# A hybrid decoder layer: steps of the recurrence, the convolution and its norm given out a slot or an operation apart, and small diagonals made on ScalarE

## The chip, the cores and the metric

The kernel runs on one core of a Trainium2 chip. The metric is device microseconds of one execution. A core has TensorE (PE; its weight loads are shown as PEld), VectorE (DVE), ScalarE (ACT), GpSimd (POOL) and SyncE (SP, which starts the transfers here). Each engine works through its own instructions in the order in which they stand; an instruction waits for semaphores of others, and all behind it on that engine wait with it. The matrix products accumulate in PSUM banks; everything else lies in SBUF.

## The reference

One layer on 512 tokens of 1024 channels, all in fp32. Three sub-layers follow one another: a SwiGLU block (inner width 2816, added at half weight), a token mixer, and a second SwiGLU block. Each takes `u = x*(1+scale)+shift` and gives `x <- LayerNorm(alpha*x + w*(1+gate)*f(u))`; scale, shift and gate come from a conditioning vector c. The mixer is where most of the change lies:

```python
proj = u @ w_in                                   # 6 parts of 1024
xr, gr, conf_in, gate_a, gate_b = jnp.split(proj, IN_SPLITS, axis=-1)
xr = causal_depthwise_conv(xr, rnn_conv_w, rnn_conv_b)            # 4 taps
hr = rg_lru(xr, ...)                              # two 128x128 products a head, then a scan
ya = (hr * jax.nn.gelu(gr)) @ rnn_w_proj
glu = conf_in[..., :D_CONV] * jax.nn.sigmoid(conf_in[..., D_CONV:])
hb = causal_depthwise_conv(glu, conf_dw_w, conf_dw_b)             # 31 taps
hb = jax.nn.silu(layer_norm(hb, conf_ln_g, conf_ln_b))
yb = hb @ conf_w_proj
out = (jax.nn.sigmoid(gate_a) * ya + jax.nn.sigmoid(gate_b) * yb) @ mix_w_out
```

The recurrence of `rg_lru` is `h_t = a_t*h_(t-1) + sqrt(1-a_t^2)*(i_t*x_t)`, with `a = exp(-8 softplus(-lambda) r)` and sigmoid gates r and i.

## The kernel before, in words

**Tiling.** Channels lie on the 128 partitions, the 512 tokens in the free dimension, so 1024 channels are eight chunks. Every fp32 product is made of three in a faster 32-bit format: high by high (L240), low by high (L241), high by low (L242). A group of one output chunk is eight chunks of weights by three products, 24 matmuls of 128x512. A weight slab comes by transfer into `raw` (two buffers); ScalarE casts the high part `whi` (L141), and the low part `wlo = raw - whi` (L145) is made on VectorE, or on GpSimd in the boundaries and the mixer (`lo_engine`). These are made four and three groups ahead (`HI_AHEAD`, `LO_AHEAD`). Activations are split the same way into `Uh`, `Ul` or `Hh`, `Hl`.

**Stages.** Startup; FFN1; boundary l1; mixer; boundary l2; FFN2; `finish` (l3 and the output). A boundary makes the last four chunks of the sub-layer's output in two halves of 256 tokens each (`Tail`; tiles `l1t`, `l2t`, `l3t`), and meanwhile the LayerNorm of the half that is done. That norm sums over channels by a product with a constant matrix (`l_rs` L317, `l_mean`), takes the inverse deviation `l_y` on GpSimd, spreads it over a diagonal matrix (`l_dg`, `diagonals`, L341), and broadcasts it by a product with ones (`l_rs` L448).

**The mixer.** It goes in four pairs of chunks. In each pair come two groups `xr` (evicted by ScalarE at L1049, and three taps on VectorE at L1053, the third of which frees the PSUM bank), the recurrence of the pair before (`rglru`: four `ri` products, then steps on VectorE, L989, L996, L1000, L1002, L1006, and ScalarE, L983, L992, L993, L997), `cb` and `ca` (the convolution's input), and two groups `gr`. Then follow 16 gate groups (`gate` into `ma` and `sb`), eight groups `ya`, eight groups `yb`. The 31-tap convolution is 30 VectorE operations per chunk (`cv`, L841) on an accumulator in PSUM; ScalarE starts it (L821) and copies it out (L846). Two accumulators are under way at a time. When all eight are out, `conv_norm` makes their LayerNorm: the sum over channels (`lc_sum`, then `lc_mu` on TensorE, L880), centring (L888), squares (L890), their sum (L894), `lc_y`, `lc_dg` (L341), `lc_rs` on TensorE (L908), scaling (L914), SiLU (L918).

**What sets the order.** The program is written out by hand, engine by engine in the order of the Python calls. Before each group, `slot()` gives out the work that was deferred for that slot (`defer(n, f)`: n slots later), then the casts ahead. Each half group is a `checkpoint()`, which first gives out the `quick` list (an entry `(n, f)` waits n further checkpoints) and then, in `background()`, spends a budget of credit on the convolution's taps and, when there are none, on the list `later`. Nothing reorders the instructions afterwards on an engine.

## Time and profile before

| | |
|---|---|
| median of 3 runs | 1182.73 us (1182.71 to 1182.8) |
| the profiled execution | 1182.73 us, of which its span 1180.9 us |
| TensorE busy | 1154.6 us |
| VectorE busy | 749.1 us |
| ScalarE busy | 434.0 us |
| GpSimd busy | 216.6 us |
| boundary l1, mixer, boundary l2 | from about 345 us, 425 us and 770 us of the span |

In a row of a timeline stand the start, the duration, the engine, the line, the operation, the tile written and those read, their shape, and in brackets the idle time before it with what ended it. A start is counted from the beginning of the span. In a row of windows stand the stretch and its length, the busy time of PE, PEld, DVE, ACT and POOL with the number of instructions, the clock that TensorE was granted (1.00 is full), the share of the transfer engines and GB/s.

### The profile page before, as it was taken

The page shows a single profiled execution, that of the slowest core. Times are in us where ns is not written, and L with a number is a line of the kernel's source. Part 1 is how long each engine was busy: PE and PEld are TensorE (multiplying, and loading weights), DVE is VectorE, ACT ScalarE, POOL GpSimd, SP SyncE. Part 2 cuts the span into 40 slices and gives each one's busy share as a digit, 9 for nine tenths or more (in the row PEclk, how much of TensorE's full clock was granted, in tenths as well). Part 3 has the DMA queues.
Part 4 walks back from the last instruction along what each step waited for, and adds up shares of the span by engine and source line. Part 5 has one row for each costly group of instructions (what it writes and reads, how often), then busy time and mean ns, then how long its engine had stood idle before and what let it go on. Part 6 is the DMA issues. An engine that isn't in the chain of part 4 may idle for free.

```text
span 1180.9 us, 13555 instructions
## 1 busy us (share of the span) xinstructions
PE 1154.6 (98%) x5527; PEld 970.4 (82%) x5527; DVE 749.1 (63%) x1030; ACT 434.0 (37%) x557; POOL 216.6 (18%) x112
## 2 busy tenths in 40 slices
PE   8999999999999999998999999999999999999996
PEld 5888888888888988887788878889888888888886
DVE  7887767732359596998999665596433232433266
ACT  4532122322323635566653442225322122222223
POOL 3200000000003554353536440022300000000002
PEclk9999999999999999998999999999999999999998
DMA  9787666422322222332233222221422321322212
GB/s 371 268 344 281 261 266 244 170 103 107 107 72 108 72 81 81 107 113 75 81 107 112 103 72 107 85 94 37 143 75 103 107 93 59 134 107 75 103 36 72
DMA packets 30318, 151.64 MB, mean 128 GB/s; under 512 B 3376, under 2 KB 5424, under 8 KB 18480
## 3 DMA queue, kind: packets, MB, share of 16 engines
q1 hardware_dynamic: 30256, 150.78, 34.9%
q8 instruction: 43, 0.70, 0.2%
q14 instruction: 19, 0.16, 0.0%
HBM read 148.67 MB, written 2.10 MB: 128 GB/s over the span
## 4 chain that ended last, share of the span: by engine, by line
PE 83%; DVE 9%; issue 3%; ACT 2%; POOL 1%; DMA 1%; SPq 0%; POOLq 0%; ACTq 0%; DVEq 0%
PE g L240 6%; PE u L240 6%; PE g L242 6%; PE u L242 6%; PE g L241 6%; PE u L241 6%; PE y L240 6%; PE y L241 6%; PE y L242 6%; PE st L759 4%; PE gate L240 2%; PE gate L242 2%; PE gate L241 2%; DVE cv L841 2%; PE yb L241 1%
## 5 line engine op out<-in xcount | busy, mean ns | idle before, releaser
L145 POOL TENSOR_TENSOR wlo<-raw,whi 128x1024 fp32r<-128x1024 f32 (+1 forms) x69 | 170.2, 2482 | 555.4 <-ACT whi L141 555.4
L141 ACT CAST whi<-raw 128x1024 fp32r<-128x1024 f32 (+2 forms) x204 | 205.4, 1021 | 151.9 <-DMA raw<-in_wide 116.0
L841 DVE SCALAR_TENSOR_TENSOR cv<-glu,prm,cv 128x511 f32<-128x511 f32 (+14 forms) x240 | 159.0, 729 | 12.5 <-ACT cv L821 12.5
L145 DVE TENSOR_TENSOR wlo<-raw,whi 128x1024 fp32r<-128x1024 f32 (+1 forms) x135 | 158.2, 1190 | 4.7 <-ACT whi L141 4.7
L689 DVE TENSOR_TENSOR h<-u,h 128x512 f32<-128x512 f32 x38 | 26.3, 691 | 204.7 <-PE u L242 204.7
L241 PE MATMUL y<-Hl,whi 128*128 128x512 f32 x320 | 124.5, 389 | 0.0
L242 PE MATMUL y<-Hh,wlo 128*128 128x512 f32 x320 | 124.5, 389 | 0.0
L240 PE MATMUL y<-Hh,whi 128*128 128x512 f32 x320 | 124.5, 389 | 0.0
L240 PE MATMUL g<-Uh,whi 128*128 128x512 f32 x304 | 118.3, 389 | 0.0
L241 PE MATMUL g<-Ul,whi 128*128 128x512 f32 x304 | 118.3, 389 | 0.0
L242 PE MATMUL g<-Uh,wlo 128*128 128x512 f32 x304 | 118.3, 389 | 0.0
L240 PE MATMUL u<-Uh,whi 128*128 128x512 f32 x304 | 118.3, 389 | 0.0
L241 PE MATMUL u<-Ul,whi 128*128 128x512 f32 x304 | 118.3, 389 | 0.0
L242 PE MATMUL u<-Uh,wlo 128*128 128x512 f32 x304 | 118.3, 389 | 0.0
L141 ACT CAST Hh<-h 128x512 fp32r<-128x512 f32 x44 | 27.0, 620 | 178.1 <-DVE h L689 178.1
L257 DVE SCALAR_TENSOR_TENSOR ada<-ada,silu_c 128x1024 f32<-128x1024 f32 x72 | 86.6, 1224 | 4.8 <-DMA ada<-in_ada 4.7
L242 PEld LDWEIGHTS y<-Hh,wlo 128*128 128x128 f32 x320 | 60.1, 188 | 12.5
L240 PEld LDWEIGHTS y<-Hh,whi 128*128 128x128 f32 x320 | 60.1, 188 | 12.5
L241 PEld LDWEIGHTS y<-Hl,whi 128*128 128x128 f32 x320 | 60.1, 188 | 12.5
L334 POOL TENSOR_TENSOR l_y<-l_va,half 128x2 f32<-128x2 f32 x5 | 3.5, 706 | 359.3 <-DVE l_va L333 359.3
L685 ACT ACTIVATE h<-g 128x512 f32<-128x512 f32 x38 | 22.7, 597 | 120.4 <-PE g L242 120.4
L242 PEld LDWEIGHTS g<-Uh,wlo 128*128 128x128 f32 x304 | 57.1, 188 | 11.9
(260 smaller groups left out, 2333.3 us busy)
## 6 DMA issues: line engine op xcount, KB each, us to landing
raw<-in_wide SPq DMA_DIRECT2D x92, 1024.0 KB, 4.8
ada<-in_ada SPq DMA_DIRECT2D x72, 512.0 KB, 7.3
raw<-in_six SPq DMA_DIRECT2D x8, 768.0 KB, 4.1
straw<-in_start SPq DMA_DIRECT2D x8, 512.0 KB, 8.9
X<-in_xT SPq DMA_DIRECT2D x8, 256.0 KB, 9.0
out_y<-X SPq DMA_DIRECT2D x8, 256.0 KB, 2.2
raw<-in_rg SPq DMA_DIRECT2D x4, 256.0 KB, 2.6
silu_c<-in_c SPq DMA_DIRECT2D x1, 512.0 KB, 3.5
```

Of the source, the lines that this page charges most:

```text
L141: self.nc.scalar.copy(out=out, in_=src)
L145: (engine or self.nc.vector).tensor_tensor(out=out, in0=src, in1=hi.bitcast(F32), op=ALU.subtract)
L240: t.matmul(ps, lhsT=w[0], rhs=x[0], start=first, stop=False)
L241: t.matmul(ps, lhsT=w[0], rhs=x[1], start=False, stop=False)
L242: t.matmul(ps, lhsT=w[1], rhs=x[0], start=False, stop=last)
L257: self.nc.vector.scalar_tensor_tensor(out=raw, in0=raw, scalar=1.0, in1=self.sc, op0=ALU.mult, op1=ALU.mult, accum_out=self.mod[:, j : j + 1])
L334: self.nc.gpsimd.tensor_tensor(out=y, in0=va, in1=self.half[:, :nb], op=ALU.pow)
L685: self.nc.scalar.activation(out=h, in_=pg, func=AF.Silu)
L689: self.nc.vector.tensor_tensor(out=h, in0=pu, in1=h, op=ALU.mult)
L759: nc.tensor.matmul(ps[i], lhsT=w[k][a][:, i * P : (i + 1) * P], rhs=self.U[b][:, k, :], start=k == 0 and (a, b) == (0, 0), stop=k == KC - ...
L841: self.nc.vector.scalar_tensor_tensor(out=acc[:, n:], in0=glu[:, : T - n], scalar=self.col("conf_dw_w", c, NTAP - 1 - n), in1=acc[:, n:], ...
```

## The change

Five things are done. (1) In `ln_front`, at the group m = 3, the fourth `wlo` of the tail that follows is asked for at once. (2) The tails' diagonals are made by ScalarE, one 128x128 activation for each block, two for a half; in `finish` the diagonal of the second half stands ahead of a subtraction, and one output operation goes from ScalarE to GpSimd. (3) A convolution that has had its last tap is copied out two convolution steps later, and only then is the next one begun. (4) The recurrence's four steps become seven, a slot apart, with the scan a checkpoint behind the square root. (5) In `conv_norm` centring, squares and sums, and later scaling and SiLU, are given out in turn, and `lc_rs` a checkpoint later.

```diff
     def diagonals(self, nm, y, scalar=False):
         nb = y.shape[1]
         dg = self.pair(f"{nm}_dg")[:, 0, :].rearrange("p (a b) -> p a b", a=4)[:, :nb, :]
+        if scalar:
+            for i in range(nb):
+                self.nc.scalar.mul(out=dg[:, i, :], in_=self.ident, mul=y[:, i : i + 1])
+            return dg
         self.nc.vector.tensor_tensor(out=dg, in0=self.ident.unsqueeze(1).broadcast_to([P, nb, P]),
...
             def diagonal(self_, h):
-                st[h]["dg"] = self.diagonals(f"{name}{h}", st[h]["y"])
+                st[h]["dg"] = self.diagonals(f"{name}{h}", st[h]["y"], scalar=True)
...
-        out(0, 3, (act, act))
+        out(0, 3, (act, pool))
+        t.diagonal(1)
         t.sub(1, 0)
-        t.diagonal(1)
         t.broadcast(1)
...
             self.group(ps, w, x)
+            if m == 3:
+
+                self.lo_to(self.cur + 3)
             if m == 2:
...
             self.after.pop(self.steps)()
-        ready = [a for a in self.active if self.active_from[a[0]] <= self.steps] or self.active
+        a = self.ending.pop(self.steps, None)
+        if a in self.active:
+            self.conv_end(a)
+            while self.waiting and len(self.active) < 2:
+                self.conv_begin()
+        live = [a for a in self.active if a[3] < NTAP - 1]
+        if not live:
+            self.conv_end(self.active[0])
+            return True
+        ready = [a for a in live if self.active_from[a[0]] <= self.steps] or live
...
         if n == NTAP - 1:
-            self.nc.scalar.copy(out=self.conv_out(c), in_=acc)
-            self.active.remove(a)
-            self.done.append(c)
-            p = c // 2
-            if {2 * p, 2 * p + 1} <= set(self.done) and p < 3:
-                self.after[self.steps + 3] = lambda: self.conv_sum(p)
+
+            self.ending[self.steps + 2] = a
         return True
+
+    def conv_end(self, a):
+        c, _, acc, _ = a
+        self.nc.scalar.copy(out=self.conv_out(c), in_=acc)
+        self.active.remove(a)
+        self.done.append(c)
+        p = c // 2
+        if {2 * p, 2 * p + 1} <= set(self.done) and p < 3:
+            self.after[self.steps + 3] = lambda: self.conv_sum(p)
...
         def centre(p):
             v.tensor_tensor(out=CV[p], in0=CV[p], in1=self.over(st["mu"], 2), op=ALU.subtract)
+
+        def square(p):
             st[f"q{p}"] = self.pair(f"lc_q{p}")
             nc.scalar.activation(out=st[f"q{p}"], in_=CV[p], func=AF.Square)
+
+        def gather(p):
+            v.tensor_tensor(out=st["q0"], in0=st["q0"], in1=st[f"q{p}"], op=ALU.add)
+        self.later(1.14, lambda: centre(0))
         for p in range(4):
-            self.later(1.14, lambda p=p: centre(p))
-            if p:
-                self.later(1.14, lambda p=p: v.tensor_tensor(out=st["q0"], in0=st["q0"], in1=st[f"q{p}"], op=ALU.add))
+            if p < 3:
+                self.later(1.14, lambda p=p: centre(p + 1))
+            self.later(0.0, lambda p=p: square(p))
+            if p > 1:
+                self.later(1.14, lambda p=p: gather(p - 1))
+        self.later(1.14, lambda: gather(3))
...
-            self.quick.append((0, bc))
+            self.quick.append((1, bc))
...
-        def a():
+        def gated():
             v.tensor_tensor(out=xc, in0=xc, in1=i_, op=ALU.mult)
+
+        def decay():
...
-        def b():
+        def power():
             v.scalar_tensor_tensor(out=th, in0=i_, scalar=1.0, in1=th, op0=ALU.add, op1=ALU.mult)
+
+        def root():
             s.activation(out=th, in_=th, func=AF.Sqrt)
-
-        def c():
+            self.quick.append((1, scan))
+
+        def scan():
             v.tensor_tensor(out=xc, in0=xc, in1=th, op=ALU.mult)
...
-        def e():
+        def out():
             v.tensor_tensor(out=i_, in0=i_, in1=gg, op=ALU.mult)
-            self.hi(hi, i_)
-            self.defer(1, lambda: self.lo(lo, i_, hi))
-
-        for n, fn in enumerate((a, b, c, e)):
-            self.defer(n + 2, fn)
+
+        for n, fn in enumerate((gated, decay, power, root, out, lambda: self.hi(hi, i_), lambda: self.lo(lo, i_, hi))):
+            self.defer(n + 1, fn)
```

How the instructions of an engine stand before and now is shown at three places; line numbers of the changed kernel are its own (L868 is the copy of L846, L828 the start of L821, L1088 the eviction of L1049, L857 the tap of L841, L1025 the multiplication of L989).

ScalarE, the fourth pair of the mixer, before. `xc` is the eviction of the first `xr` group, `Hh<-i` the cast of the recurrence's result of an earlier pair, `CV<-cv` a finished convolution copied out, `cv<-glu` the start of the next.

```order
L1065 ACTIVATE gg_3699<-gr 128x512 x2
L141 CAST Hh<-i_3751 128x1024
L141 CAST whi_3972<-raw_3855 128x1024
L141 CAST whi_3976<-raw_3931 128x1024
L846 COPY CV_3999<-cv_3456 128x512
L1049 ACTIVATE xc_3967<-xr,prm 128x512
L821 ACTIVATE cv_4015<-glu_3280,prm 128x512
L846 COPY CV_3999<-cv_3460 128x512
L821 ACTIVATE cv_4020<-glu_3280,prm 128x512
L983 ACT_TABLE_LOAD
```

The same place now:

```order
L1104 ACTIVATE gg_3701<-gr 128x512 x2
L141 CAST whi_3973<-raw_3857 128x1024
L141 CAST whi_3977<-raw_3930 128x1024
L1088 ACTIVATE xc_3969<-xr,prm 128x512
L868 COPY CV_4016<-cv_3459 128x512
L828 ACTIVATE cv_4018<-glu_3282,prm 128x512
L868 COPY CV_4016<-cv_3477 128x512
L828 ACTIVATE cv_4023<-glu_3282,prm 128x512
L141 CAST Hh<-i_3753 128x1024
L1018 ACT_TABLE_LOAD
```

The eviction `xc` has moved ahead of both copies and of the cast, which stands behind the copies and starts.

VectorE, the same pair a little later, before: `Hl<-i` and `Hl<-xc` are the low parts of the recurrence's result and of the new `xc`, `xc<-xc,i` the gate multiplication of the recurrence.

```order
L145 TENSOR_TENSOR Hl<-i_3751,Hh 128x1024
L866 TENSOR_TENSOR lc_sum<-CV_3442,CV_3999 128x1024
L841 SCALAR_TENSOR_TENSOR cv_4015<-glu_3280,prm,cv_4015 128x510
L1053 SCALAR_TENSOR_TENSOR xc_3967<-xr,prm,xc_3967 128x511
L841 SCALAR_TENSOR_TENSOR cv_4020<-glu_3280,prm,cv_4020 128x510
L1053 SCALAR_TENSOR_TENSOR xc_3967<-xr,prm,xc_3967 128x510
L841 SCALAR_TENSOR_TENSOR cv_4015<-glu_3280,prm,cv_4015 128x509
L1053 SCALAR_TENSOR_TENSOR xc_3967<-xr,prm,xc_3967 128x509
L841 SCALAR_TENSOR_TENSOR cv_4020<-glu_3280,prm,cv_4020 128x509
L145 TENSOR_TENSOR Hl<-xc_3967,Hh 128x1024
L841 SCALAR_TENSOR_TENSOR cv_4015<-glu_3280,prm,cv_4015 128x508
L989 TENSOR_TENSOR xc_3698<-xc_3698,i_4027 128x1024
```

Now:

```order
L887 TENSOR_TENSOR lc_sum<-CV_3457,CV_4016 128x1024
L857 SCALAR_TENSOR_TENSOR cv_4018<-glu_3282,prm,cv_4018 128x509
L1092 SCALAR_TENSOR_TENSOR xc_3969<-xr,prm,xc_3969 128x510
L857 SCALAR_TENSOR_TENSOR cv_4023<-glu_3282,prm,cv_4023 128x509
L1092 SCALAR_TENSOR_TENSOR xc_3969<-xr,prm,xc_3969 128x509
L857 SCALAR_TENSOR_TENSOR cv_4018<-glu_3282,prm,cv_4018 128x508
L145 TENSOR_TENSOR Hl<-i_3753,Hh 128x1024
L1025 TENSOR_TENSOR xc_3700<-xc_3700,i_4029 128x1024
L145 TENSOR_TENSOR Hl<-xc_3969,Hh 128x1024
L857 SCALAR_TENSOR_TENSOR cv_4023<-glu_3282,prm,cv_4023 128x508
```

The low part `Hl<-i` has moved behind the taps of `xc`, and the gate multiplication between the two low parts.

VectorE at the end of FFN1, ahead of the tail, before. `l_s` and `l_q` are the sums of X and of its squares, the five `drv` rows small columns of eight; the product `l1t` waits for the second `wlo`.

```order
L145 TENSOR_TENSOR wlo_2426<-raw_2324,whi_2390 128x1024
L665 SCALAR_TENSOR_TENSOR X<-y,drv,X 128x512
L679 TENSOR_TENSOR l_s_2455<-X 128x1024
L680 TENSOR_TENSOR l_q_2454<-l_q_2454,l_q_2456 128x1024
L295 SCALAR_TENSOR_TENSOR drv<-mod,prm 128x8
L296 SCALAR_TENSOR_TENSOR drv<-mod,prm 128x8
L297 TENSOR_TENSOR drv<-drv,mod 128x8
L298 TENSOR_SCALAR drv<-prm 128x8
L299 TENSOR_SCALAR drv<-prm 128x8
L145 TENSOR_TENSOR wlo_2466<-raw_2324,whi_2424 128x1024
L366 SCALAR_TENSOR_TENSOR X<-l1t_2468,drv,X 128x256
```

Now:

```order
L145 TENSOR_TENSOR wlo_2426<-raw_2324,whi_2390 128x1024
L145 TENSOR_TENSOR wlo_2453<-raw_2324,whi_2424 128x1024
L672 SCALAR_TENSOR_TENSOR X<-y,drv,X 128x512
L686 TENSOR_TENSOR l_s_2457<-X 128x1024
L687 TENSOR_TENSOR l_q_2456<-l_q_2456,l_q_2458 128x1024
L295 SCALAR_TENSOR_TENSOR drv<-mod,prm 128x8
```

The second `wlo` has moved directly behind the first, and the update, the sums and the `drv` rows behind it.

More of the change, by code (lines that the diff above doesn't have):

```diff
@@ L110, in __init__ @@
         self.active_from, self.last_step, self.steps = {}, {}, 0
-        self.done, self.after = [], {}
+        self.done, self.after, self.ending = [], {}, {}
         self.CV = [None] * 4
@@ L335, in deviation, with diagonals @@
         return y
-    def diagonals(self, nm, y):
+    def diagonals(self, nm, y, scalar=False):
         nb = y.shape[1]
         dg = self.pair(f"{nm}_dg")[:, 0, :].rearrange("p (a b) -> p a b", a=4)[:, :nb, :]
+        if scalar:
+            for i in range(nb):
+                self.nc.scalar.mul(out=dg[:, i, :], in_=self.ident, mul=y[:, i : i + 1])
+            return dg
         self.nc.vector.tensor_tensor(out=dg, in0=self.ident.unsqueeze(1).broadcast_to([P, nb, P]),
@@ L914, in scale, with silu @@
             v.tensor_tensor(out=CV[p], in0=CV[p], in1=self.over(st["rs"], 2), op=ALU.mult)
+        def silu(p):
             for j in range(2):
@@ L925, in conv_norm @@
         ends = []
+        self.later(1.14, lambda: scale(0))
         for p in range(4):
-            self.later(1.14, lambda p=p: scale(p))
+            if p < 3:
+                self.later(1.14, lambda p=p: scale(p + 1))
+            self.later(0.0, lambda p=p: silu(p))
         self.until(free)
```

## The prediction

> **What bounds the kernel now.** I read the page first, then the waits of TensorE, then the timelines of the four engines around each wait.
>
> ```profile
> span 1180.9 us, 13555 instructions
> PE 1154.6 (98%) x5527; PEld 970.4 (82%) x5527; DVE 749.1 (63%) x1030; ACT 434.0 (37%) x557; POOL 216.6 (18%) x112
> ```
>
> TensorE is busy for 98% of the span, and the change takes no product from it. What can be won is the time in which it waits, or runs at a lower clock; what can be lost is a new wait. The profiled execution took 1182.73 us, which is also the median of the three runs; 1.83 us of it lie around the span.
>
> ```profile
> PE l_rs L448 <- DVE l_dg L341: 4.6, 3, 2.8
> PE cb L240 <- DVE xc L1053: 3.5, 1, 3.5
> PE lc_rs L908 <- DVE lc_dg L341: 1.4, 1, 1.4
> PE l_rs L317 <- DVE l_sum L381: 1.1, 2, 0.6
> PE l1t L242 <- DVE wlo L145: 1.0, 1, 1.0
> PE l2t L242 <- DVE wlo L145: 1.0, 1, 1.0
> PE gate L240 <- ACT ma L1078: 0.7, 1, 0.7
> ```
>
> The columns are the total, the number of waits and the longest, in us. These seven lines add to 13.3 us, and every part of the change stands beside one of them: the weight half `wlo` at the boundaries, the broadcast diagonals `l_dg`, the recurrent branch's `xc` that holds back `cb`, and the broadcast `lc_rs`. I go through them in that order of the program, and follow each to the wait that comes after it, for a wait that is removed only lets TensorE reach the next one sooner.
>
> **Boundaries (l1, and l2 alike).** The fourth `wlo` of the tail now goes to VectorE ahead of the update of X, the sums and five small `drv` operations.
>
> ```profile
> 358.25 0.28 PE L241 MATMUL l1t<-Hl,whi 128*128 128x256 f32 x1
> 359.53 0.38 PE L242 MATMUL l1t<-Hh,wlo 128*128 128x256 f32 x1 [1.00 <-DVE wlo L145]
> ...
> 365.01 0.28 PE L242 MATMUL l1t<-Hh,wlo 128*128 128x256 f32 x1
> 365.13 0.95 PE L317 MATMUL l_rs<-inv_d,l_sum 128*128 128x1 f32 x8
> ```
>
> Two of these products stand 0.12 us apart (365.01 to 365.13), so 358.25 to 359.53 costs 1.28 - 0.12 = 1.16 us. That goes whole: by VectorE's order the half comes right behind the third one. But the reduction `l_rs` at 365.13 waits for VectorE too.
>
> ```profile
> 349.27 1.22 DVE L145 TENSOR_TENSOR wlo<-raw,whi 128x1024 fp32r<-128x1024 f32 x1
> ...
> 353.46 2.37 DVE L295 SCALAR_TENSOR_TENSOR drv<-mod,prm 128x8 f32<-128x8 f32 x1
> ...
> 355.94 2.25 DVE L297 TENSOR_TENSOR drv<-drv,mod 128x8 f32<-128x8 f32 x1
> ...
> 362.45 0.48 DVE L366 SCALAR_TENSOR_TENSOR X<-l1t,drv,X 128x256 f32<-128x256 f32 x1 [0.41 <-PE l1t L242]
> ...
> 364.59 0.42 DVE L382 TENSOR_TENSOR l_sum<-l_q 128x256 f32<-128x256 f32 x1
> 353.26 4.91 POOL L145 TENSOR_TENSOR wlo<-raw,whi 128x1024 fp32r<-128x1024 f32 x2 [302.27 <-ACT whi L141]
> ```
>
> Two `drv` operations of eight columns take over 2.2 us each, exactly while GpSimd's two `wlo` of 4.91 us run. The moved half pushes X, the square on ScalarE, the two `whi` casts behind it and so GpSimd's start by about 1.14 us each (the half's 1.22 less overlap); VectorE is then let go at the same time as before, 359.4. Its chain to `l_sum` gains only the 0.41 us at 362.45, and `l_sum` is there at 365.01 - 0.41 = 364.60. TensorE, 1.16 us earlier, stands at 363.97 and waits about 0.7. So of 1.16 us about 0.4 reach the reduction; the bounds are 0.4 and 1.16 (if the `drv` operations slip in ahead of GpSimd).
>
> ```profile
> 367.71 2.61 DVE L341 TENSOR_TENSOR l_dg<-prm,l_y 128x256 f32<-128x256 f32 x1 [0.25 <-POOL l_y L334]
> ...
> 370.38 0.70 PE L448 MATMUL l_rs<-l_dg,ones 128*128 128x256 f32 x2 [0.89 <-DVE l_dg L341]
> ...
> 371.35 0.63 ACT L371 ACTIVATE l_sq<-X 128x512 f32<-128x512 f32 x1 [5.05 <-DVE X L366]
> 381.64 1.05 PE L317 MATMUL l_rs<-inv_d,l_sum 128*128 128x1 f32 x8 [0.50 <-DVE l_sum L381]
> ```
>
> The diagonal moves to ScalarE as two activations of 128x128. ScalarE is idle from 366.3 to 371.35, so they start at once. No row has that shape; 0.63 us for 128x512 is the nearest, so the pair costs at most 1.26, and I take 0.8, since a quarter of the elements will not take the whole 0.63. It is done near 368.5 (at worst 369.0), with TensorE there at 369.49 - 0.4 = 369.1: the 0.89 us wait goes. The later `l_sum` wait of 0.5 stays: VectorE has work without a pause there, its chain starts from the broadcast, and it moves with TensorE, or by the 2.61 us of `l_dg` at most. I take 0.4 + 0.9 + 0.3 = 1.6 us for a boundary, **3.2** for both, between 2.0 (0.4 + 0.6 each) and 5.0 (all three waits: 1.0 + 0.9 + 0.6 each).
>
> **The recurrence, pair 3.**
>
> ```profile
> 540.50 0.39 PE L241 MATMUL xr<-Ul,whi 128*128 128x512 f32 x1
> 540.73 0.39 PE L242 MATMUL xr<-Uh,wlo 128*128 128x512 f32 x1
> 544.59 0.76 PE L240 MATMUL cb<-Uh,whi 128*128 128x512 f32 x1 [3.47 <-DVE xc L1053]
> ...
> 537.60 2.00 ACT L141 CAST whi<-raw 128x1024 fp32r<-128x1024 f32 x2
> 539.79 0.59 ACT L846 COPY CV<-cv 128x512 f32<-128x512 f32 x1 [0.20 <-DVE cv L841]
> 540.28 0.78 ACT L1049 ACTIVATE xc<-xr,prm 128x512 f32<-128x512 f32 x1
> ...
> 541.10 0.75 DVE L1053 SCALAR_TENSOR_TENSOR xc<-xr,prm,xc 128x511 f32<-128x511 f32 x1 [1.33 <-ACT xc L1049]
> ...
> 543.70 0.74 DVE L1053 SCALAR_TENSOR_TENSOR xc<-xr,prm,xc 128x509 f32<-128x509 f32 x1
> 543.00:551.00 8.00, 6.41 (x16) 5.10 (x17) 5.51 (x8) 7.42 (x11) 1.56 (x2) 0.57 0.03 10
> ```
>
> `cb` needs the bank of the first `xr`, which is free when the third of three taps (543.70) is done. Products of this size stand 0.23 us apart, so the gap costs 3.86 - 0.23 = 3.63 us; and the window row behind it (PE, PEld, DVE, ACT, POOL, granted clock) has the clock at 0.57. At full clock its cb products would have taken 6.41 x 0.57 = 3.65 of the 6.41 busy us, so 2.8 us are lost again.
>
> ScalarE evicts `xc` only at 540.28, behind the cast of the recurrence's result, two `whi` casts and a copy of the convolution. The change puts that cast and the copies behind the eviction, so ScalarE can have it near 534 to 536, as soon as the group is done. Then VectorE decides. It has no pause up to 539.8; the three taps stand in the same place between its convolution taps. Without the 1.33 us wait they start at 539.8 and end 1.3 us earlier, at 543.1. The wait at `cb` is then 3.63 - 1.3 = 2.3 us (bounds 0.9 and 3.2, as VectorE's moved multiplications and their waits for GpSimd come out), and I take it that the clock stays up. That is 1.3 + 2.8 = 4.1 us, and the `gate` wait of 0.7 goes since ScalarE's backlog is shorter: 4.8 us.
>
> TensorE then comes 4.8 us earlier, at 657.8, to the convolution's mean, which needs all of VectorE's work on the convolution:
>
> ```profile
> 526.02 2.51 DVE L1000 TENSOR_TENSOR xc<-xc,th 128x1024 f32<-128x1024 f32 x1
> ...
> 605.02 1.26 DVE L1000 TENSOR_TENSOR xc<-xc,th 128x1024 f32<-128x1024 f32 x1
> ...
> 550.52 0.75 DVE L1053 SCALAR_TENSOR_TENSOR xc<-xr,prm,xc 128x511 f32<-128x511 f32 x1 [2.49 <-ACT xc L1049]
> ...
> 657.45 0.69 DVE L876 TENSOR_TENSOR lc_sum<-lc_sum 128x512 f32<-128x512 f32 x1
> 525.04 5.74 POOL L145 TENSOR_TENSOR wlo<-raw,whi 128x1024 fp32r<-128x1024 f32 x2 [3.19 <-ACT whi L141]
> ...
> 662.63 1.02 PE L880 MATMUL lc_mu<-lc_sum,inv_d 128*128 128x512 f32 x2
> ```
>
> Before, `lc_sum` is ready at 658.14 and TensorE 4.5 us later. Now VectorE sets the mean. It saves the 1.33 us at 541.10, but its second pause (550.52, for the second `xc`) grows: ScalarE's cast (1.0, half of the `whi` row) now stands ahead of the sigmoids that precede that `xc`, and VectorE comes to the pause 1.33 sooner. That makes 2.5 + 1.0 + 1.3 = 4.8 us in place of 2.5 + 1.3 = 3.8, so 1.0 late. A second loss: a multiplication of two tiles takes 1.26 us alone and 2.51 while GpSimd has a `wlo` in hand. The order now sets the gate multiplication `xc<-xc,i` between the two subtractions `Hl`, three such operations behind one another close to GpSimd's work; I count one more of them blocked, 1.25 us. So `lc_sum` comes at 658.1 + 1.0 + 1.25 = 660.4, and TensorE waits 2.6 us. The recurrence brings 4.8 - 2.6 = **2.2 us**. Bounds: VectorE 3.8 us earlier, both pauses gone, leaves all 4.8; three or four blocked operations more leave 4.8 - 2.6 - 3.75 = -1.6.
>
> [...]
>
> **The norm of the convolution.** `lc_rs` goes from the next checkpoint to the one after it.
>
> ```profile
> 685.12 1.10 PE L908 MATMUL lc_rs<-lc_dg,ones 128*128 128x512 f32 x2 [1.43 <-DVE lc_dg L341]
> ```
>
> Twelve products, 12 x 0.23 = 2.7 us, come in ahead of it, so TensorE gets there at 683.7 + 2.7 = 686.4, when `lc_dg` has been ready since 685: 1.4 us by the wait, **1.6** with the refilling of TensorE's pipeline that each wait shows on top (3.63 for 3.47 above). What follows is later by about 1.3 us (686.4 - 685.1): the four multiplications by `lc_rs`, the SiLUs and the splits, until the `yb` products. These come eight groups of products after the gates, and operations given out one apart no longer wait for each other's answer, so I take it as hidden; if that cover is gone, 1.3 us come back and 0.3 is left. The lower bound is 0.3, the upper 1.6.
>
> **The tail.**
>
> ```profile
> 1170.87 1.48 DVE L341 TENSOR_TENSOR l_dg<-prm,l_y 128x256 f32<-128x256 f32 x1 [0.19 <-POOL l_y L421]
> ```
>
> Here everything is on the path. ScalarE's pair in 0.8 instead of VectorE's 1.48 brings **0.6 us** (0.2 if it costs 1.26; 1.1 if two activations take 0.4). One output operation goes from ScalarE to GpSimd ahead of the subtractions there, which costs those and not the diagonal; I count it as nothing, and 0.5 at worst.
>
> **Sum.** 3.2 + 2.2 + 1.6 + 0.6 = 7.6 us. 1182.7 - 7.6 = **1175.1 us**. The extra ScalarE activations (six pairs) stand in ScalarE's idle time, for it is busy for 37% of the span.
>
> **The rivals.** (a) VectorE keeps up. The first pause vanishes and ScalarE's earlier evictions let it finish `lc_sum` before 657.8. For it speaks that every pause that I have quoted of VectorE in pair 3 is for ScalarE; against it that VectorE is otherwise without a pause and its work is not made less. The recurrence then brings 4.8 and the sum 10.2 us: 1172.5. With the boundaries' upper end (5.0) it is 1170.7.
>
> (b) VectorE is the bound for the whole of the mixer, and the wait at `cb` only moves to `lc_mu`. The wait there is over 3.5 us and the clock falls as it did behind the 3.47 us: 4.8 - 3.7 - 2.8 = -1.7 us. Sum 3.2 - 1.7 + 1.6 + 0.6 = 3.7: 1179.0. For it speaks that my own wait of 2.6 us is only 0.9 short of one that took the clock down. [...]
>
> (c) Slower. GpSimd's `wlo` and VectorE's two-tile operations block each other all along the four pairs of the recurrence, because gate multiplication and both subtractions now come in one block in each. If in each pair three operations are held 1.25 us more, VectorE is 15 us later at `lc_sum`: 658.1 + 15 - 1.3 = 671.8, TensorE waits 14 us and loses 2.8 at the lower clock. Mixer 4.8 - 14 - 2.8 = -12, sum -12 + 5.4 = -6.6: 1189.3. It decides from about 7 us of lateness on (4.8 + 5.4 - 2.8 = 7.4, less the 0.3 that it waits without any). Against it: only half of such operations met GpSimd before (2.51 and 1.26 are the two kinds), and GpSimd is busy for 18% of the span.
>
> (d) It doesn't do what it says: ScalarE's pair costs as much as the blocked 2.61, or ScalarE is held by a `whi` cast of 1.0 us at that moment, `l_dg` waits stay, and the convolution's copies, two steps later, hold up the same bank as before. Then 1.6 us of `lc_rs` and 0.8 of the boundaries' halves are left: 2.4 us, 1180.3.
>
> **Chances.** The forecast (1173 to 1177) 0.42; (a) 0.20; (b) 0.20; (d) 0.09; (c) 0.09. What a measurement here can tell from no change is 0.2%, 2.4 us: faster is below 1180.4, slower above 1185.1. Forecast, (a) and (b) are faster, and a part of (d): 0.84. No change is the rest of (d) and the mild end of (c): 0.08. Slower is 0.08. The range runs from (a) with the boundaries' good end, 1170, to (b) with 1.3 us of `lc_rs` lost, 1180.3: **1170.0 to 1180.5**. It leaves out (c), a half of (d) and the far end of (a). The likeliest case's own range is 1173 to 1177.
>
> **What would show it.** The boundaries: the 1.0 us waits for `wlo` and the 0.9 us waits for `l_dg` are gone, and a wait of about 0.7 us stands at the first `l_rs` instead, with `drv` operations of over 2 us still there. The recurrence: `xc` on ScalarE 4 to 6 us ahead of its place, the wait at `cb` near 2.3 us, and a clock of 1.00 in that window; at `lc_mu` a wait of 2 to 3 us for `lc_sum`. The norm: no wait at `lc_rs`, and none at the first `yb`. The tail: two activations of about 0.4 us in place of 1.48. Wrong would be: a wait at `cb` as long as before with the clock down (my step from ScalarE to VectorE falls), no wait at `lc_mu` (rival a), a wait over 3.5 us there (rival b), or two-tile operations above 2 us in every pair (rival c).

## The result and the profile after

| | median, us | runs | against the kernel before, run beside it, 95% interval |
|---|---|---|---|
| before | 1182.76 | 4 (1182.71 to 1184.02) | |
| the changed kernel | 1175.95 | 4 (1174.23 to 1176.75) | 0.9935 (0.9922 to 0.9949) |
| the changed kernel a second time | 1174.75 | 5 (1173.77 to 1176.47) | 0.9925 (0.9912 to 0.9939) |

Predicted were 1175.1 us, from 1170.0 to 1180.5. The sum was right to a microsecond; two groups of its terms were not, and they nearly cancelled, which is luck. The page of the changed kernel:

```profile
span 1175.0 us, 13568 instructions
PE 1152.5 (98%) x5527; PEld 969.9 (83%) x5527; DVE 742.0 (63%) x1024; ACT 437.1 (37%) x568; POOL 219.7 (19%) x113
```

The waits of TensorE in the changed kernel, total, number and longest in us:

```profile
PE st L781 <- ACT silu_c L91: 5.9, 1, 5.9
PE lc_mu L901 <- DVE lc_sum L897: 3.7, 1, 3.7
PE l_rs L452 <- ACT l_dg L343: 2.1, 1, 2.1
PE st L766 <- ACT Uh L759: 1.2, 1, 1.2
PE st L766 <- DVE Ul L145: 1.2, 1, 1.2
PE l_rs L317 <- DVE l_sum L385: 1.1, 4, 0.4
```

The waits for `wlo`, for `xc` at `cb`, for `lc_dg` and for `ma` are gone; of the three for `l_dg` the tail's is left, with 2.1 us in place of 2.8. One long new wait stands at `lc_mu`, 3.7 us, and two short ones among the four for `l_sum`, at the first `l_rs` of each boundary. The two `st` waits of 1.2 us belong to the start of the program, which the change doesn't touch. Timeline of TensorE, the same products of the start, first in the kernel before, then in the changed one:

```profile
17.23 2.14 PE L759 MATMUL st<-Uh,sthi 128*128 128x512 f32 x8
```

```profile
18.61 1.66 PE L766 MATMUL st<-Uh,sthi 128*128 128x512 f32 x6
```

This execution began 1.38 us later. That is chance: in the 14 profiles of this document the start lies anywhere in a stretch of 1.7 us, and the kernel before itself, 1182.76 us here, has medians of 1183.6 to 1184.1 us beside the kernels below. The next table takes it out. "Start to start" there means the time from the start of the last product ahead of a wait to the start of the first behind it, less the usual spacing of two products.

| stage | forecast, us won | measured in the profile | from |
|---|---|---|---|
| boundaries l1 and l2 | 3.2 | 4.2 | waits below, start to start |
| mixer up to `lc_mu` | 4.8 | 7.3 | waits at `cb` and `gate` gone, 3.63 + 2.81 + 0.82 |
| the wait at `lc_mu` | -2.6 | -3.9 | |
| lower clock behind it | 0 | -2.9 | spacing 0.43 for 0.23 |
| `lc_rs` | 1.6 | 1.7 | |
| tail | 0.6 | 0.8 | |
| sum | 7.6 | 7.2 | |
| the start | | -1.4 | |

7.2 - 1.4 = 5.8, against 1180.9 - 1175.0 = 5.9 us between the spans.

The changed kernel where `cb` waited, timelines of ScalarE, VectorE and GpSimd:

```profile
532.26 0.78 ACT L1088 ACTIVATE xc<-xr,prm 128x512 f32<-128x512 f32 x1 [2.96 <-PE xr L242]
...
523.96 1.36 DVE L1041 TENSOR_TENSOR xc<-xc,th 128x1024 f32<-128x1024 f32 x1
525.36 2.34 DVE L1043 TENSOR_TENSOR_SCAN i<-r,xc 128x512 f32<-128x512 f32 x2
...
528.86 3.05 DVE L1047 TENSOR_TENSOR i<-i,gg 128x1024 f32<-128x1024 f32 x1
...
534.97 0.74 DVE L1092 SCALAR_TENSOR_TENSOR xc<-xr,prm,xc 128x511 f32<-128x511 f32 x1
...
516.12 8.12 POOL L145 TENSOR_TENSOR wlo<-raw,whi 128x1024 fp32r<-128x1024 f32 x3 [1.72 <-ACT whi L141]
528.43 5.76 POOL L145 TENSOR_TENSOR wlo<-raw,whi 128x1024 fp32r<-128x1024 f32 x2 [4.19 <-ACT whi L141]
```

ScalarE evicts `xc` as soon as the products are done, as forecast. The first tap, though, comes at 534.97, not near 539: VectorE reached it early. The multiplication by the root (1.36) and both scans (2.34) fell between two stretches of GpSimd's work, from 524.2 to 528.4, where before they took 2.51 and 4.41 us. The product behind them (L1047) met the second stretch in their stead, 3.05 us for 1.21 before. And at the mean, TensorE and the window behind it:

```profile
658.32 2.04 PE L901 MATMUL lc_mu<-lc_sum,inv_d 128*128 128x512 f32 x2 [3.70 <-DVE lc_sum L897]
656.00:666.00 10.00, 7.68 (x20) 5.49 (x21) 6.39 (x7) 7.44 (x10) 8.30 (x4) 0.66 0.22 71
...
657.48 0.69 DVE L897 TENSOR_TENSOR lc_sum<-lc_sum 128x512 f32<-128x512 f32 x1
```

`lc_sum` is done at 658.17, before it was 658.14. VectorE is no sooner, TensorE is, and waits; then the clock falls, to 0.66 of full speed as the mean of that window. `lc_mu` itself is one product in plain fp32: 2.04 us here at half clock, 1.02 us in the kernel before at full clock, where a product of the same size in the faster format took 0.39 us (L240).

### The profile page after: what moved, and what is told of

The parts are those of the page before. It is cut to its first block, busy times and chain, and to the rows that moved or that the text cites. A ratio compares the mean times of both kernels' runs of the same rounds, so it can differ in the third digit from the quotient of the medians.

```text
span 1175.0 us, 13568 instructions
## 1 busy us (share of the span) xinstructions
PE 1152.5 (98%) x5527; PEld 969.9 (83%) x5527; DVE 742.0 (63%) x1024; ACT 437.1 (37%) x568; POOL 219.7 (19%) x113
## 4 chain that ended last, share of the span: by engine, by line
PE 80%; DVE 16%; ACT 2%; issue 1%; DMA 1%; SPq 0%; POOL 0%; DVEq 0%; POOLq 0%; ACTq 0%
DVE cv L857 7%; PE y L240 6%; PE g L240 6%; PE u L240 6%; PE g L241 6%; PE y L241 6%; PE u L241 6%; PE y L242 6%; PE g L242 6%; PE u L242 6%; PE st L766 4%; PE yb L240 1%; PE yb L241 1%; PE yb L242 1%; PE ya L240 1%; PE ya L242 1%
## 5 line engine op out<-in xcount | busy, mean ns | idle before, releaser
L145 POOL TENSOR_TENSOR wlo<-raw,whi 128x1024 fp32r<-128x1024 f32 (+1 forms) x69 | 172.9, 2523 | 548.5 <-ACT whi L141 548.5
L857 DVE SCALAR_TENSOR_TENSOR cv<-glu,prm,cv 128x511 f32<-128x511 f32 (+14 forms) x240 | 158.4, 729 | 13.1 <-ACT cv L828 13.1
L242 PE MATMUL y<-Hh,wlo 128*128 128x512 f32 x320 | 124.5, 389 | 0.0
L240 PE MATMUL y<-Hh,whi 128*128 128x512 f32 x320 | 124.5, 389 | 0.0
L240 PE MATMUL g<-Uh,whi 128*128 128x512 f32 x304 | 118.3, 389 | 0.0
L242 PE MATMUL g<-Uh,wlo 128*128 128x512 f32 x304 | 118.3, 389 | 0.0
L240 PE MATMUL u<-Uh,whi 128*128 128x512 f32 x304 | 118.3, 389 | 0.0
L242 PE MATMUL u<-Uh,wlo 128*128 128x512 f32 x304 | 118.3, 389 | 0.0
L242 PEld LDWEIGHTS y<-Hh,wlo 128*128 128x128 f32 x320 | 60.1, 188 | 12.6
L240 PEld LDWEIGHTS y<-Hh,whi 128*128 128x128 f32 x320 | 60.1, 188 | 12.5
L242 PEld LDWEIGHTS g<-Uh,wlo 128*128 128x128 f32 x304 | 57.2, 188 | 12.0
```

The lines of the kernel that those rows point to most:

```text
L145: (engine or self.nc.vector).tensor_tensor(out=out, in0=src, in1=hi.bitcast(F32), op=ALU.subtract)
L240: t.matmul(ps, lhsT=w[0], rhs=x[0], start=first, stop=False)
L242: t.matmul(ps, lhsT=w[1], rhs=x[0], start=False, stop=last)
L857: self.nc.vector.scalar_tensor_tensor(out=acc[:, n:], in0=glu[:, : T - n], scalar=self.col("conf_dw_w", c, NTAP - 1 - n), in1=acc[:, n:], ...
```

## The experiments

**The tails alone, the mixer's order alone, the norm alone.** The kernel before with one group of the change each.

```diff
 # tails (parts 1 and 2)
+                st[h]["dg"] = self.diagonals(f"{name}{h}", st[h]["y"], scalar=True)
+            if m == 3:
+                self.lo_to(self.cur + 3)
 # mixer (parts 3 and 4): conv_step and rglru of the changed kernel
 # norm (part 5): conv_norm of the changed kernel
+            self.quick.append((1, bc))
```

> The kernel before with parts 1 and 2 of the change alone (the early wlo, the diagonals on ScalarE). Theory: the parts add, and each boundary gives what the trace of the changed kernel shows for it, about 2.1 us each (the third wait, l_sum, stays near 0.5 us, and a new one of about 0.35 us stands at the first l_rs), the tail 0.8: 5.0 us, 1177.7 us. Rival: the boundaries' gain is given back in the mixer, because VectorE's chain to cb there doesn't move with it: then the wait at cb grows from 3.5 to 5.6 us, only l2 and the tail are left, 2.9 us, 1179.9 us.

> The kernel before with parts 3 and 4 alone (the convolution's end two steps later, the recurrence in seven steps). Theory: VectorE's work sets the mean of the convolution. The 3.5 us wait at cb with its slow clock (6.4 us together) and the gate wait of 0.7 go, TensorE comes 7.2 us earlier to lc_mu, and waits there 3.5 to 3.9 us for lc_sum and loses 2.9 at the lower clock: gain 0 to 0.8 us, 1182 to 1182.7 us. Rival: the mixer's parts are worth what I forecast for them, 2.2 us, with no lower clock at lc_mu: 1180.5 us.

> The kernel before with part 5 alone (the norm of the convolution in turns, lc_rs a checkpoint later). Theory: the 1.4 us wait at lc_rs goes and nothing comes back at yb: 1.6 us won against the kernel before. Rival: the norm ends later and yb waits for it: nothing won.

| | median, us | ratio to before, 95% interval |
|---|---|---|
| tails alone | 1179.85 | 0.9966 (0.9954 to 0.9978) |
| mixer's order alone | 1182.19 | 0.9985 (0.9976 to 0.9994) |
| norm alone | 1182.20 | 0.9988 (0.9978 to 0.9998) |

In us these are 4.0, 1.8 and 1.4, together 7.2; the whole change has 7.7 and 8.9 by its two ratios. So the parts add, within intervals of about 1 us to either side for each. The mixer's order, which is most of the change, brings little: 7.3 us are removed there, and come back for the most part at `lc_mu`, as a wait of 3.7 us and a lower clock. The tails alone won 4.0 us where 5.0 were expected.

The tails alone show something else. Waits of TensorE and windows of that kernel, behind `cb` and behind `gate`:

```profile
PE cb L240 <- DVE xc L1060: 3.5, 1, 3.5
PE gate L240 <- ACT ma L1085: 3.4, 1, 3.4
...
543.00:551.00 8.00, 7.23 (x32) 6.04 (x33) 5.51 (x7) 6.63 (x10) 1.94 (x1) 1.00 0.01 2
581.00:589.00 8.00, 6.19 (x20) 4.96 (x21) 8.00 (x13) 7.65 (x11) 6.46 (x3) 0.79 0.37 131
```

The wait at `cb` is 3.5 us as before, but no lower clock follows it (1.00, before 0.57), and the wait at `gate` is 3.4 in place of 0.7, with a lower clock behind it (0.79) that the kernel before doesn't have there. The kernel with the norm alone, the same two places:

```profile
PE gate L240 <- ACT ma L1092: 1.9, 1, 1.9
...
543.00:551.00 8.00, 6.55 (x22) 5.31 (x23) 5.52 (x7) 7.31 (x10) 1.56 (x2) 0.79 0.03 12
```

Taken start to start, the clock behind `cb` and the wait at `gate` cost 2.81 + 0.82 before, 1.61 + 2.02 here and 0.08 + 3.59 with the tails alone: 3.63, 3.63 and 3.67 us. What TensorE saves at the clock it waits for at `gate`, since ScalarE's `ma` there comes when VectorE and ScalarE are done, not when TensorE is. My price of 2.8 us for the lower clock of the kernel before was thus right only together with the `gate` wait.

**The steps of the recurrence, or the end of the convolution, undone.**

```diff
 # without part 4: rglru of the kernel before
...
-        for n, fn in enumerate((gated, decay, power, root, out, lambda: self.hi(hi, i_), lambda: self.lo(lo, i_, hi))):
-            self.defer(n + 1, fn)
+        for n, fn in enumerate((a, b, c, e)):
+            self.defer(n + 2, fn)
 # without part 3: conv_step of the kernel before
...
-            self.ending[self.steps + 2] = a
+            self.nc.scalar.copy(out=self.conv_out(c), in_=acc)
...
```

> The changed kernel with the recurrence in its four steps of before (part 4 undone), all else kept. Theory: the cast of the recurrence's result stands ahead of the xc eviction on ScalarE again and the multiplication by the root meets GpSimd's wlo (2.5 us in place of 1.3); a wait of 1 to 4 us stands at cb again. What TensorE loses there it no longer loses at lc_mu, since VectorE sets that: the time stays within 2 us of the changed kernel. Rival: the convolution's end (part 3) alone clears cb: no wait there, and the wait at lc_mu stays at 3.7.

> The changed kernel with the convolution's end as before (part 3 undone), the recurrence in seven steps kept. Theory: one copy of the convolution stands ahead of the xc eviction on ScalarE, and that copy waits for VectorE's last tap; the wait at cb is 0.5 to 3 us, less than before by the cast that is gone. The time stays within 2 us of the changed kernel, as VectorE sets lc_mu. Rival: the split alone clears cb, as without part 4 it doesn't: no wait at cb.

Without part 4: 1181.19 us, 0.9977 (0.9967 to 0.9986), by the ratios 5 to 6 us slower than the whole change, where within 2 us was expected. Without part 3: 1173.35 us, 0.9915 (0.9900 to 0.9929), not to be told from the whole. Waits of TensorE without part 4, and ScalarE and VectorE ahead of them:

```profile
PE gate L240 <- ACT ma L1113: 3.9, 1, 3.9
PE cb L240 <- DVE xc L1088: 2.7, 1, 2.7
...
579.45 1.05 ACT L141 CAST Hh<-i 128x1024 fp32r<-128x1024 f32 x1 [9.04 <-DVE i L1041]
...
583.71 0.60 ACT L1113 ACTIVATE ma<-gate 128x512 f32<-128x512 f32 x1
...
525.46 2.51 DVE L1035 TENSOR_TENSOR xc<-xc,th 128x1024 f32<-128x1024 f32 x1
528.01 4.42 DVE L1037 TENSOR_TENSOR_SCAN i<-r,xc 128x512 f32<-128x512 f32 x2
```

Both waits are back, and no wait at `lc_mu`. ScalarE stands 9.04 us before the cast `Hh<-i`, and the eviction of `ma`, on which TensorE's bank hangs, stands behind that cast. Missed here was that two waits of TensorE follow from one late VectorE, and that the time lost there is more than `lc_mu` gives back: TensorE got to `lc_mu` after `lc_sum`. Without part 3 there is no wait at `cb`, so the split clears it alone, as the rival said (without part 4 it was still 2.7 us), and the wait at `lc_mu` is 2.3 us in place of 3.7: with the copies two steps later `lc_sum` comes 1.4 us later in these profiles, and nothing is won by them.

**The cast alone.** Part 4 undone, but the cast given out a slot later as in the change.

```diff
-            self.hi(hi, i_)
-            self.defer(1, lambda: self.lo(lo, i_, hi))
-        for n, fn in enumerate((a, b, c, e)):
+        for n, fn in enumerate((a, b, c, e, lambda: self.hi(hi, i_), lambda: self.lo(lo, i_, hi))):
             self.defer(n + 2, fn)
```

> The changed kernel with the recurrence in its four steps of before, but the cast of its result (and the low part) given out a slot later, as in the changed kernel. Beside the kernel with all of part 4 undone this moves the cast alone. Theory: the gate wait (3.9 us there) came because the eviction of ma stood on ScalarE behind that cast, which waits for VectorE's product of the recurrence: it goes, with its 1.7 us of lower clock. At cb ScalarE is early now, but VectorE with its blocked multiplication and scan (2.5 and 4.4 us) reaches the taps only 0.5 us sooner than with the cast early: a wait of 2.0 to 2.5 us is left at cb (2.7 there). TensorE is then nearer to lc_sum, and waits 1 to 2.5 us at lc_mu: 1173 to 1176 us. Rival 1: the cast alone clears cb too, as the seven steps did. Rival 2: the order of VectorE's steps clears both, and the cast nothing: a gate wait of over 3 us and 1181 us again.

1185.29 us, 1.0012 (1.0003 to 1.0021): slower than the kernel before by about 1.4 us, where 1173 to 1176 us were expected. The `gate` wait is gone, as the theory of the cast says. But the rest went the other way:

```profile
PE lc_mu L901 <- DVE lc_sum L897: 5.5, 1, 5.5
PE cb L240 <- DVE xc L1086: 4.9, 1, 4.9
...
525.98 2.51 DVE L1035 TENSOR_TENSOR xc<-xc,th 128x1024 f32<-128x1024 f32 x1
528.53 6.58 DVE L1037 TENSOR_TENSOR_SCAN i<-r,xc 128x512 f32<-128x512 f32 x2
...
525.00 12.31 POOL L145 TENSOR_TENSOR wlo<-raw,whi 128x1024 fp32r<-128x1024 f32 x4 [3.19 <-ACT whi L141]
```

ScalarE, no longer standing at the cast, made the `whi` casts sooner; GpSimd therefore had four `wlo` in one stretch, 12.31 us, and both scans met it: 6.58 us in place of 4.42. The same goes for both scans of the first and the third pair; in all, the eight scans up to the mean take 24.2 us here and 15.8 in the changed kernel. VectorE reached `lc_sum` about 10 us later than there, counted from the start. An engine made faster has moved a collision onto another engine's path. That is rival (c) of the prediction, in three of the four pairs, and it shows that the seven steps win by where VectorE's operations fall between GpSimd's.

**GpSimd's `wlo` left out in the mixer.** The products that read `wlo` (L242) read `whi` in its place, so this kernel leaves out the low parts of the mixer's weights; the number of products is the same.

```diff
+            if self.skip_lo:
+                self.los.append(self.his[j])
+                continue
             t = self.lop.tile([P, 1024], F32R, tag="lo", name=f"wlo{j}")
```

> The changed kernel with GpSimd's wlo in the mixer left out (the low by high products use the high part of the weights, so the mixer's numbers are not the reference's); the products are as many as before. Theory: VectorE's operations with two SBUF inputs are held by GpSimd's wlo; without it each of the 28 in the mixer takes its time alone (1.2 to 1.3 us), VectorE has 10 to 13 us less to do up to lc_sum, and the wait at lc_mu with its lower clock is gone: 6.7 us won against the changed kernel. Rival: VectorE is paced by ScalarE's evictions, so lc_sum comes less than 2 us sooner, and a wait of 2 us or more is left at lc_mu.

1169.53 us, 0.9878 (0.9865 to 0.9892), by the two ratios 6.7 and 5.6 us faster than the changed kernel, where 6.7 was expected. VectorE's groups up to the mean, in the changed kernel and then here (count, busy us, mean ns):

```profile
L1043 DVE TENSOR_TENSOR_SCAN i<-r,xc 128x512 f32<-128x512 f32 x8 | 15.8, 2010 | 0.1
L1047 DVE TENSOR_TENSOR i<-i,gg 128x1024 f32<-128x1024 f32 x4 | 8.5, 2113 | 0.0
```

```profile
L1047 DVE TENSOR_TENSOR_SCAN i<-r,xc 128x512 f32<-128x512 f32 x8 | 9.4, 1212 | 0.1
L1051 DVE TENSOR_TENSOR i<-i,gg 128x1024 f32<-128x1024 f32 x4 | 4.9, 1220 | 0.0
...
644.34 0.69 DVE L901 TENSOR_TENSOR lc_sum<-lc_sum 128x512 f32<-128x512 f32 x1
654.42 3.48 DVE L913 TENSOR_TENSOR CV<-CV,lc_mu 128x1024 f32<-128x1024 f32 x3 [9.39 <-PE lc_mu L905]
```

`lc_sum` is done 13.1 us sooner (645.03 for 658.17; 12.1 with the two starts taken out), and it is VectorE that now waits for TensorE, 9.39 us. The theory stands: the time for which GpSimd holds VectorE up sets the mean, and with it what the mixer's part of the change could win. Of the eight scans of the changed kernel five took 1.2 us, the mean of the eight here, and the three that stood beside a `wlo` from their start 3.3 to 3.4 us. The convolution's taps, with an operand in PSUM, show nothing of it: all 240 took 0.70 to 0.76 us there. The rival, that VectorE is paced by ScalarE's evictions, falls.

**The mean later on TensorE.** If `lc_sum` can't come sooner, `lc_mu` can stand later among products that don't need it. LC_MEAN is the number of checkpoints by which `lc_mu` is put off, LC_SUMS the same for `lc_tok`, the product that sums the squares.

```diff
-LC_MEAN, LC_SUMS = 4, 2
+LC_MEAN, LC_SUMS = 5, 2      # and 6, 2; and 6, 3
```

> The changed kernel with LC_MEAN 5 in place of 4: lc_mu stands one checkpoint (12 products, 2.7 us) later on TensorE. Theory: lc_sum comes no later, so the wait falls from 3.7 to about 1.0 us, the clock stays at full speed, and 2.7 + 2.9 = 5.6 us are won against the changed kernel: 1170.4 us. Rival 1: the clock falls here whatever the wait: 2.7 us, 1173.3 us. Rival 2: the norm behind the mean is what limits, and yb waits for it: no gain, 1176 us.

> The changed kernel with LC_MEAN 6: lc_mu two checkpoints, 5.4 us, later on TensorE. Theory: no wait at lc_mu and no lower clock, 3.8 + 2.9 = 6.7 us won against the changed kernel, 1169.3 us; the norm's end keeps 1 to 2 us ahead of yb. Rival 1, the clock falls anyway: 1172.1 us. Rival 2, the norm limits: yb waits 1 us or more, and no more is won than with one checkpoint.

> The changed kernel with LC_MEAN 6 and LC_SUMS 3: lc_mu two checkpoints and lc_tok three checkpoints later on TensorE. Theory: both waits, for lc_sum and for lc_q, are gone, with no lower clock: against the kernel with LC_MEAN 6 alone the 2.8 us wait at lc_tok and its 1.7 us of lower clock are won, 4.5 us, 1169.3 us; against LC_MEAN 5 alone 1.2 us, 1170.3 us. Rival: the norm is now too late for yb, whose first products wait for Ul: 1 to 3 us come back, 1171 to 1173 us.

| LC_MEAN, LC_SUMS | median, us | ratio to before, 95% interval | wait at `lc_mu` | at `lc_tok` |
|---|---|---|---|---|
| 4, 2 (the change) | 1175.95 and 1174.75 | 0.9935, 0.9925 | 3.7 | none |
| 5, 2 | 1171.47 | 0.9896 (0.9883 to 0.9910) | 1.0 | none |
| 6, 2 | 1173.77 | 0.9918 (0.9905 to 0.9932) | none | 2.8 |
| 6, 3 | 1169.64 | 0.9879 (0.9866 to 0.9893) | none | none |

One checkpoint later is worth 4.6 us by the first ratio ((0.9935 - 0.9896) x 1183), 3.4 by the second; 5.6 were expected, with the clock loss of 2.9 that the second profile below doesn't have in full. A second one alone loses part of it (1169.3 us were expected), since the sum of squares then isn't ready for `lc_tok`: the wait has only gone on, with its lower clock. With `lc_tok` later as well both waits are gone, nothing stands at `yb`, and the time is the 1169.3 to 1170.3 us expected.

**Small operations out of GpSimd's way.** In each boundary the five `drv` operations behind the sums of the first half.

```diff
         t.combine(0)
+        cc = cols()          # affine_cols, before: ahead of boundary()
+        gg, bb = cc[:2]
```

> The kernel with LC_MEAN 6 and LC_SUMS 3, and the five small drv operations of each boundary behind the sums of its first half instead of ahead of the updates of X. Theory: two of the five stood for over 2.2 us each because GpSimd's wlo ran; behind the sums they meet no GpSimd work and take 0.15 us each, VectorE reaches l_sum of the first half over 1 us sooner, and the wait at the first l_rs (0.35 us) goes; with what the second half gains, 0.4 to 0.9 us a boundary: 0.8 to 1.8 us for both. Rival: these rows are slow for themselves, whatever GpSimd does: then they are as long in their new place, hold up the deviation, and 2 to 4 us a boundary are lost.

1169.20 us, 0.9875 (0.9862 to 0.9888), the fastest; against the run beside it (1169.64, 0.9879) the gain is too small to be told by the times. Start to start, and with their starts taken out (1.08 us apart), the profile gives 0.9 us, where 0.8 to 1.8 were expected. The same operation in the changed kernel and in this one:

```profile
355.93 2.37 DVE L295 SCALAR_TENSOR_TENSOR drv<-mod,prm 128x8 f32<-128x8 f32 x1
```

```profile
364.99 0.16 DVE L295 SCALAR_TENSOR_TENSOR drv<-mod,prm 128x8 f32<-128x8 f32 x1
```

Of its 2.37 us 2.2 were GpSimd's. The rival, slow for itself, falls.

**The changed kernel again.**

> The changed kernel once more, as the base for the three beside it, and for the spread. Theory: the start differs by up to 1.4 us from one profile to the next (the first products behind the conditioning vector stood at 16.8, 18.2, 18.1, 18.3, 18.2 and 17.3 us so far), and the clock does not fall in every execution behind a wait of 3.5 us, as at cb of the kernel with the tails alone, where nothing was lost behind 3.5 us. Then the wait at lc_mu is 3.7 us again, to 0.1, and the time lies between 1174 and 1177 us, by whether the clock falls behind it. Rival: the wait itself differs between executions.

1174.75 us, from 1173.77 to 1176.47. Its profile has the wait at `lc_mu` at 3.7 us again, and less lower clock behind it:

```profile
656.00:666.00 10.00, 8.50 (x28) 6.28 (x29) 7.75 (x8) 6.62 (x8) 9.13 (x4) 0.83 0.30 104
```

0.83 for 0.66; start to start 1.7 us are lost in place of 2.9. With the start (0.8 us earlier here) that is the 2.0 us between the two spans. The runs of the three kernels without a long wait (LC_MEAN 5; 6 and 3; the `drv` operations moved) scatter by 0.2 to 1.2 us.

## Why the prediction came out right, and where its steps were wrong

**Boundaries: mechanism right, 3.2 forecast, 4.2 measured.** In the changed kernel:

```profile
365.57 1.05 PE L317 MATMUL l_rs<-inv_d,l_sum 128*128 128x1 f32 x8 [0.19 <-DVE l_sum L385]
...
358.41 2.26 DVE L297 TENSOR_TENSOR drv<-drv,mod 128x8 f32<-128x8 f32 x1
...
368.25 0.69 ACT L343 ACTIVATE l_dg<-prm,l_y 128x128 f32<-128x128 f32 x2 [1.86 <-POOL l_y L334]
```

The new wait at the first `l_rs` is there, and so is its cause, the two `drv` rows of over 2 us. It is 0.19 us in the row (0.35 start to start), not 0.7: I had taken the second of the two `l_sum` operations (L382) as what releases the product, but the first four columns need only the first, 0.33 us sooner. ScalarE's pair of diagonals takes 0.69 us, 0.8 was taken.

**The wait at `cb`: 2.3 us forecast, none measured.** The step that failed is "It has no pause up to 539.8; the three taps stand in the same place between its convolution taps". Their place in the order is nearly the same, but how long the operations ahead of them take hangs on when GpSimd runs. Multiplication and scans took 3.7 us in place of 6.9, of which the product behind them gave 1.8 back. In the pair before it went alike (3.6 for 6.8 us, and 1.8 back), and VectorE came out of it 2.0 us sooner against TensorE (its last `glu` product ahead of this place starts at 517.63 for 520.36; TensorE is 0.7 us sooner there). With 0.6 us less at L1034 and the ScalarE wait of 1.33 the first tap came 5.4 us sooner against TensorE, and that cleared `cb`. The collision was known from the rows and was counted on the side of the losses only.

**The wait at `lc_mu`: 2.6 us forecast, 3.7 measured, and 2.9 of lower clock.** That VectorE sets the mean was right, and the experiment without GpSimd's `wlo` shows why. `lc_sum` came out 0.8 us later against the boundary than before, 2.25 were forecast. The pause for the second `xc` grew much as forecast, from 2.49 to 5.13 us where 4.8 was taken:

```profile
545.41 0.75 DVE L1092 SCALAR_TENSOR_TENSOR xc<-xr,prm,xc 128x511 f32<-128x511 f32 x1 [5.13 <-ACT xc L1088]
```

The collisions with GpSimd were moved, and none was saved on the whole: from 425 to 660 us the scans and seven of the two-tile operations (in the lines of the changed kernel L1025, L1034, L1041, L1047, both `Hl`, the first `lc_sum`) take VectorE 54.5 us in the kernel before, 55.9 in the changed one and 40.0 without `wlo`, which is 1.4 us more where 1.25 was forecast. Not counted in the forecast was that VectorE waits less for the cast `Hh` ahead of `Hl<-xc`, 0.5 us in place of 2.1. TensorE was there sooner than forecast, by the wait at `cb` that fell away, and so waited longer. The lower clock was rival (b)'s. Taken together the mixer up to there gave 7.3 - 3.9 - 2.9 = 0.5 us, 2.2 were forecast; the boundaries' surplus of 1.0 made up for most of it. That the sum came within a microsecond is therefore luck, and so is a part of the measured 1175.95: the same kernel's second profile lost 1.2 us less at the clock.

**`lc_rs` and the tail** came as forecast: 1.7 for 1.6, with no wait at `yb` (the norm alone won 1.4 us), and 0.8 for 0.6, the pair of diagonals 0.69 in place of 1.48. Start to start a wait cost 0.16 us more than its row at `cb` before (3.63 for 3.47), at the first `l_rs` of the changed kernel (0.35 for 0.19) and at its `lc_mu` (3.86 for 3.70); that this is a refilling of TensorE's pipeline is the prediction's reading and is not shown.

**The rivals.** (a), VectorE keeping up, is refuted by the 3.7 us wait, though its half at `cb` came true. (b) came true at `lc_mu` by the sign given for it, a wait over 3.5 us with the clock down; as the wait at `cb` went whole, the mixer gave 0.5 us and not the -1.7 of (b). It is the reason that a change of so many steps in the mixer is worth 1.8 us there. (c) is not what this change does, and is what the cast alone does; its sign, operations above 2 us in every pair, stands in both kernels if the scans are counted, and so tells nothing. (d) falls by the waits that are gone.

**The clock.** The prediction took 2.3 us at `cb` and 2.6 at `lc_mu` to cost no clock. No run shows that as a rule: without part 3 a wait of 2.32 us at `lc_mu` brought the clock to half for 3.41 us. Behind which waits it fell, and behind which of equal length it did not, is read from the traces in the last section; that it fell for 6.83 us in one execution of the changed kernel and for 3.41 in the other is chance.

## What to carry to other kernels

A wait removed from the busiest engine is worth only what lies between it and the next result of the engine behind: look for that result's slack first (4.5 us here), and if it doesn't move, put the operation that needs it later, among work that doesn't. Where two engines hold each other up, an operation's price is its place against the other's work, not its row (two `wlo` took GpSimd 4.76 us with VectorE idle, and 5.76 us beside the product at L1047, which took 3.05 us for 1.21); moving one cast shifted collisions by which VectorE lost 10 us. An instruction that waits long should not stand ahead of one that frees a PSUM bank (without part 4 the cast waited 9.04 us, and TensorE 3.9 us at `gate`), but to move it alone is no gain for sure: the cast moved alone took its wait at `gate` away and made the kernel 1.4 us slower.

## What the runs showed of the hardware that was not expected

The length of a wait alone did not tell whether TensorE's clock fell behind it. Behind 3.47 us at `cb` the window of 8 us had 0.57, behind the same wait with the tails alone 1.00; behind 3.7 us at `lc_mu` a window of 10 us had 0.66 and 0.83 in two executions of one kernel. And a shorter wait brought it down too, without part 3, to 0.79 as the mean of the 8 us from 656 us:

```profile
656.86 1.58 PE L887 MATMUL lc_mu<-lc_sum,inv_d 128*128 128x512 f32 x2 [2.32 <-DVE lc_sum L883]
```

The clock in the traces has two values in all, 1.00 and 0.50. Between the start of the program and its tail, a stretch at 0.50 lasts 3.41 or 6.83 us, and the stretches at 1.00 between them are whole multiples of 3.41 us too (the one behind `cb` of the kernel before, 550.43 to 1171.66, is 182 of them). So in these traces the clock changed on a grid of 3.41 us, and the grid lay elsewhere against the span from one execution to another: counted in steps of 3.4133 us (621.23 / 182) from the start of the span, its edges stand 0.9 us behind a whole number of steps in the kernel before (543.61) and 2.1 us in the changed one (657.42). Three waits on their grids, each row one window of it: `cb` with the tails alone, `lc_mu` of the changed kernel, `lc_mu` of its second profile. The second number is the time in which TensorE was busy, and the clock stands behind POOL's:

```profile
538.66:542.07 3.41, 1.62 (x8) 1.00 (x6) 2.08 (x4) 2.44 (x5) 3.41 (x2) 1.00 0.19 68
542.07:545.48 3.41, 1.71 (x8) 1.46 (x9) 3.41 (x6) 3.35 (x5) 0.54 (x1) 1.00 0.04 14
545.49:548.90 3.41, 3.41 (x17) 2.83 (x16) 1.72 (x2) 3.41 (x7) 0.00 (x0) 1.00 0.00 0
...
654.01:657.42 3.41, 0.61 (x3) 0.18 (x1) 2.76 (x4) 2.41 (x4) 0.00 (x0) 1.00 0.01 2
657.43:660.84 3.41, 2.52 (x4) 1.43 (x5) 1.15 (x3) 3.05 (x5) 3.15 (x2) 0.50 0.02 5
660.84:664.25 3.41, 3.41 (x9) 2.64 (x9) 3.04 (x3) 2.60 (x3) 3.41 (x2) 0.50 0.15 24
...
654.11:657.52 3.41, 0.02 (x1) 0.06 (x1) 2.55 (x4) 3.33 (x6) 0.65 (x1) 1.00 0.01 2
657.53:660.93 3.40, 3.40 (x6) 2.08 (x7) 1.37 (x2) 2.25 (x4) 3.40 (x2) 0.50 0.02 5
660.94:664.35 3.41, 3.41 (x16) 2.77 (x15) 3.41 (x4) 2.83 (x3) 3.41 (x3) 1.00 0.36 94
```

The wait of 3.49 us with the tails alone lay across an edge, 1.79 us in one window and 1.70 in the next, and cost no clock. In the 14 profiles, from 60 to 1150 us, the clock fell behind each of the twelve windows at full clock in which TensorE stood idle for 2.20 us or more, and behind none with 1.79 us or less. It stayed down for a second window in the five cases in which the first one had 0.89 us or more of idle time, and rose behind the twelve with 0.16 or less. So the 2.32 us without part 3, which lay whole in one window, cost a window at half clock, and the 3.49 us cost nothing. What lies between 1.79 and 2.20 us, and what the small products of the tail do, isn't shown.
